# Routing weights of the PEER stage: added word by word into DRAM by indirect DMAs instead of built by one-hot products

## The chip, the core and the metric

The kernel runs on one core of one Trainium2 chip. The metric is the device time of one execution in microseconds, as a median of several executions; the profile is one execution more, recorded by the hardware profiler. A core has TensorE (PE, with a separate weight load, PEld), VectorE (DVE), ScalarE (ACT), GpSimd (POOL), SyncE (SP, which issues DMAs here) and 16 DMA engines. Each engine works through its instructions in the order of the program and waits on semaphores; it never takes a later instruction first.

## The reference, cut to what matters

One layer with three branches (differential attention, a chunk MLP, memory attention), a gate and an output projection, then PEER: every token picks 8 x 16 experts of 16384 by product keys and adds their weighted outputs. There are 320 tokens, 256 of the prompt and 64 samples.

```python
def _peer_block(xb, w_query, sub_keys, expert_u, expert_v):
    q = (xb @ w_query).reshape(tb, PEER_HEADS, 2, PEER_HALF)
    s = jnp.einsum('thpc,hpkc->thpk', q, sub_keys).astype(jnp.float32)
    s1, i1 = lax.top_k(s[:, :, 0], PEER_TOPK)
    s2, i2 = lax.top_k(s[:, :, 1], PEER_TOPK)
    ...
    top_s, top_j = lax.top_k(cand_s, PEER_TOPK)
    eidx = jnp.take_along_axis(cand_i, top_j, axis=-1)     # i1 * 128 + i2
    g = jax.nn.softmax(top_s, axis=-1).astype(xb.dtype)
    a = jax.nn.gelu(jnp.einsum('td,thkd->thk', xb, expert_u[eidx]), approximate=False)
    return jnp.einsum('thk,thkd->td', g * a, expert_v[eidx])
```

## The kernel before

**The stream.** All weights pass through one stream of *halves* of 512 KB (128 x 1024 words). SP loads a half into one of five `raw` buffers, ACT writes `hi` (the value rounded to the product format), DVE writes `lo` = `raw` - `hi`, and TensorE makes 24 products of a half: for each of 8 blocks `hi` by `xh`, `hi` by `xl`, `lo` by `xh`. There are four buffers each of `hi` and `lo`. The products of the stream stand at L359.

**PEER for the prompt.** The 256 prompt tokens are computed densely, over all 16384 experts. An Up piece (two halves of `pu`) gives 128 experts' activations for 256 tokens; four pieces are a group, with one buffer `hs` for GELU's output. There are 32 groups. The first 20 groups are written to DRAM (`hd`) and read back late. A Down piece (two halves of `pv`) takes the weighted activations `w` of two groups. 24 groups go up (192 halves) before the first Down piece; then Up and Down alternate until all 32 are up, and Down runs to the end.

**The routing weights G.** Ahead of Down, `weigh` multiplies `hs` by the weights `gg`, a table of 128 experts x 256 tokens for each piece. They come out of a DRAM array `gd`, which is filled during the first Up groups. Before, `weights_lane` runs 64 units (`g_unit`), four tokens each: DVE compares a row of 0 to 127 with the tokens' first and second key (`oa`, `ob`), GpSimd multiplies `ob` by the weight's two parts (`wH`, `wL`), TensorE makes 4 products of 128 x 256 (256 in all), ACT and DVE bring them into `st`, and SP writes `st` to `gd`, 1 MB for 16 tokens. When all units are through, SP loads `gg` from `gd`, 1 MB for two groups.

**PEER for the samples.** The 64 sample tokens use gathers: 128 indirect DMAs on GpSimd bring rows of `pur` into one of four buffers `gs` (128 rows of 4 KB), each followed by a dot product on DVE (`gs<-gs,xs`), then 128 of `pvr`, each followed by an addition into `x2s` on DVE. `idx` holds their row numbers.

**Routing.** `route_lane` finds the top 16 of the keys and of the pairs on DVE; `decode(i)` turns the results of one tile of tokens (0 and 1: prompt, 2: samples) into keys, weights and row numbers.

**What sets the order.** The program is written out by a planner (`Plan`): it keeps a clock for each engine and for DMA, with a cost for each instruction (a GpSimd gather 1.05 us, the DMA rate `RATE`, DVE's `dve_cost`, the gap `GAP` of a product), and lets the side tasks (routing, G, gathers, `weigh`) issue their instructions between the halves of the stream when its clocks say that their inputs are there. The planner's times are only used to order the instructions of each engine; on the chip every one waits on semaphores.

Of the kernel before, what the change touches and what calls it, by code (L numbers as in the profile page):

```python
# [11 lines left out]
F32 = mybir.dt.float32  # L12
# [9 lines left out]
TP = 256  # L22
# [15 lines left out]
RATE = 380e3  # L38
# [4 lines left out]
TB = 16  # L43
# [43 lines left out]
class Plan:  # L87
# [4 lines left out]
    def __init__(self):  # L92
        self.clk = {e: 0.0 for e in ("pe", "act", "dve", "pool", "dma")}
        self.task = self.main = Task(None)
        self.tasks = []
        self.done = {}
        self.uses = {}
        self.table = None

# [37 lines left out]
    def move(self, queue, out, src):  # L137

        at = max(self.last(out, True), self.last(src, False))
        if queue != "sync":  # L140
            at = self.clk[queue] = max(self.clk[queue], at) + (1.0 if queue == "pool" else 0.1)
        n = size(out) * out.shape[0] * 4
        self.clk["dma"] = max(self.clk["dma"], at) + n / RATE
        self.touch(out, self.clk["dma"] + 2.0, True)
        self.touch(src, self.clk["dma"] + 2.0, False)

    def gather(self, out, idx):
        at = self.clk["pool"] = max(self.clk["pool"], self.last(out, True), self.last(idx, False)) + 1.05
        self.clk["dma"] = max(self.clk["dma"], at) + size(out) * out.shape[0] * 4 / RATE
        self.touch(out, self.clk["dma"] + GLAT, True)  # L150
# [6 lines left out]
    def spawn(self, gen):  # L157
        self.tasks.append(Task(gen, self.task.at))
# [53 lines left out]
class Engine:  # L212
# [4 lines left out]
    def __getattr__(self, op):  # L217
        f = getattr(self.eng, op)

        def call(*a, **k):  # L220
# [4 lines left out]
            if op == "indirect_dma_start":  # L225
                p.gather(out, k["in_offset"].ap)
                return r
# [39 lines left out]
def hybrid_kernel(ctx: ExitStack, tc: tile.TileContext, ins, outs, stop=None):  # L267
# [34 lines left out]
    pool.memset(one, 1.0)  # L302
    mhalf = consts.tile([128, 1], F32, name="mhalf")
# [68 lines left out]
    class Piece:  # L372

        GAP = 0.0025
# [135 lines left out]

    s1 = ExitStack()
# [24 lines left out]
    def late_consts():  # L536
# [17 lines left out]
        dve.tensor_scalar(bgh, vec[:, V_BG:V_BG + 48], 0.5, None, op0=ALU.mult)  # L554

# [442 lines left out]
    spawn(late_consts())  # L998

# [131 lines left out]
    def open_route():  # L1131
# [5 lines left out]
        for n in ("iT0", "iT1", "wH", "wL"):  # L1137
            R[n] = p.tile([128, DN], F32R if n == "wH" else F32, name=n)
# [18 lines left out]
        spawn(weights_lane())  # L1157
# [45 lines left out]
    def wq_in(h, p):  # L1203
        def go(ps):
# [9 lines left out]
            if p == 1:  # L1214
                plan.see(sk)
                yield
                for i in range(3):
# [66 lines left out]
    def weights_lane():  # L1284
        yield from need(*[("dec", i) for i in range(3)])
        rtmp.close()
        q = open_pool(gtmp, "gtmp")
        OA = Slots(plan, q, "oa", [128, 4, 128], F32R, 3)
        OB = Slots(plan, q, "ob", [128, 4, 2, 128], F32R, 3)
        ST = Slots(plan, q, "st", [128, 128, TB], F32, 2)  # L1290
        st = None
        for t0 in range(0, DN, 4):
            if t0 % TB == 0:
                st, = yield from take(ST)
            oa, ob = yield from take(OA, OB)
            spawn(g_unit(t0, oa, ob, OA, OB, ST, st))
        while len(gdone) < DN // 4:
            yield
        gtmp.close()
        open_late()  # L1300
        mark("G")

    gdone = []
    gd = dram.tile([DN // TB, 128, 132 * TB], F32, name="gd")
    hd = dram.tile([NG, 128, GE * DN], F32, name="hd")

    def decode(i):
# [37 lines left out]
        rows = slice(0, 128) if i < 2 else slice(64, 64 + DN - TP)  # L1345
        n = rows.stop - rows.start
        if n:
            bk, = yield from take(BK)
            for a, nm in enumerate(("i0", "i1", "wt")):
                pe.transpose(bk[:, a * 128:a * 128 + n], R[nm][rows, i].rearrange("p h k -> p (h k)"), ident[rows, rows])  # L1350
            yield
            c = slice(i * 128, i * 128 + n)
            for a, nm in enumerate(("iT0", "iT1", "wH")):
                act.activation(R[nm][:, c], bk[:, a * 128:a * 128 + n], AF.Copy)
            dve.tensor_tensor(R["wL"][:, c], bk[:, 256:256 + n], R["wH"][:, c], op=ALU.subtract)
            BK.give(bk)
# [23 lines left out]

    def g_unit(t0, oa, ob, OA, OB, ST, st):

        io = cst[:, None, C_IO:C_IO + 128].to_broadcast([128, 4, 128])
        col = lambda nm: R[nm][:, t0:t0 + 4, None].to_broadcast([128, 4, 128])
# [4 lines left out]
        yield  # L1389
        b2 = yield from take(BK, BK)  # L1390
        for k in range(4):
            mm(b2[k // 2][:, (k % 2) * 256:(k % 2) * 256 + 256], oa[:, k, :], ob[:, k].rearrange("p j i -> p (j i)"),
               start=True, stop=True)
        OA.give(oa)
        OB.give(ob)
        yield
        o, work = t0 % TB, []
        for a, bk in enumerate(b2):
            v = bk.rearrange("p (t j i) -> p t j i", t=2, j=2)
            s2 = st[:, :, o + 2 * a:o + 2 * a + 2].rearrange("p i t -> p t i")  # L1400
            act.activation(s2, v[:, :, 0], AF.Copy)
            work.append((s2, v[:, :, 1], bk))
        yield
        for s2, x, bk in work:
            dve.tensor_tensor(s2, s2, x, op=ALU.add)
            BK.give(bk)
        if o == TB - 4:
            plan.see(st)
            yield
            sync.dma_start(gd[t0 // TB][:, :128 * TB], st.rearrange("p i t -> p (i t)"))  # L1410
            ST.give(st)
        gdone.append(t0)

# [10 lines left out]
    def open_late():  # L1424
        p = open_pool(late, "late")
        X["WT"] = Slots(plan, p, "w", [128, 2, 2 * GE, DN], F32R, 2)
        X["GG"] = Slots(plan, p, "gg", [128, DN // TB, 2 * GE * TB], F32, 1)

    def gathers():

        yield from need(("dec", 2))
        for src, use in (("pur", dot), ("pvr", axpy)):
            for j in range(128):
# [3 lines left out]
                spawn(use(j, gs))  # L1437
# [78 lines left out]
    def weigh():  # L1516
        for g in ORDER:
# [5 lines left out]
            h4 = hs.rearrange("p e (b t) -> p e b t", t=TB)  # L1523
            g4 = gg.rearrange("p b (e t) -> p e b t", t=TB)
            for k in range(GE + 1):
                if k < GE:
                    dve.tensor_tensor(h4[:, k], h4[:, k], g4[:, o + k], op=ALU.mult)
                    act.activation(w[:, 0, o + k, :], hs[:, k, :], AF.Copy)
                if k:
                    dve.tensor_tensor(w[:, 1, o + k - 1, :], hs[:, k - 1, :], w[:, 0, o + k - 1, :], op=ALU.subtract)  # L1530
                yield 0
# [208 lines left out]
```

## Time and profile before

| | us |
|---|---|
| median of 3 runs | 2733.84 |
| lowest and highest | 2730.56, 2739.34 |
| the profiled execution | 2734.69 |
| its span, first to last instruction | 2732.9 |
| granted TensorE clock, mean over the span | 0.985 |

The span falls into the earlier stages (0 to 1139.9), the Up groups ahead of the first Down product (1139.9 to 1797.4), the mixed and Down groups (to 2720.0), and an end of 12.9. Busy times count instructions at work; register, branch, semaphore and DMA-issuing instructions are not counted. A granted clock of 1.00 is 2.4 GHz for TensorE, the lower of its two levels is 1.2 GHz, and a mean between them is a share of time at each. A line "A <- B" among the waits is idle time of A that ended when B was done.

### The profile page before, as it was taken

How to read it: one execution, taken by the hardware profiler on the slowest of the kernel's cores; microseconds unless marked ns; L12 is line 12 of the kernel's file. 1: busy time of each engine (PE TensorE's matmuls, PEld its weight loads, DVE VectorE, ACT ScalarE, POOL GpSimd, SP SyncE). 2: the span in 40 equal slices, each digit the busy share in tenths (PEclk: the TensorE clock that was granted, in tenths of full speed). 3: DMA queues.
4: the chain of work that ended last, by engine and by line, in shares of the span. 5: the costliest groups of instructions: out<-in, count | busy, mean ns of one | idle time of the engine just before them, and what ended most of it. 6: DMA issues, size and time to landing. Idle time of an engine off the chain costs nothing. (4 is left out here: it accounts for less than half of the span.)

```text
span 2732.9 us, 49761 instructions
## 1 busy us (share of the span) xinstructions
PE 2633.5 (96%) x19824; PEld 2587.2 (95%) x19824; DVE 2024.8 (74%) x3201; ACT 1137.6 (42%) x1613; POOL 941.2 (34%) x728
## 2 busy tenths in 40 slices
PE   7999999999999999999889898999999999999998
PEld 5899989999999999999889898999999999999997
DVE  8545666344444449999999998888778888888887
ACT  4344444333333334344444444444444444344442
POOL 7423342000001222045878877422223321122122
PEclk9999999999999999999999999999999999999999
DMA  7433333444444554456777787798988888888887
GB/s 229 166 124 120 123 113 131 150 151 147 154 147 147 176 173 141 152 185 222 271 279 275 272 284 271 296 318 302 333 310 308 310 329 298 310 299 312 289 293 255
DMA packets 217560, 626.31 MB, mean 229 GB/s; under 512 B 19824, under 2 KB 74096, under 8 KB 215280
## 3 DMA queue, kind: packets, MB, share of 16 engines
q1 hardware_dynamic: 174944, 470.40, 49.1%
q0 software_dynamic: 39504, 142.24, 14.9%
q10 hardware_dynamic: 2880, 10.49, 1.0%
q8 instruction: 157, 2.57, 0.4%
q14 instruction: 75, 0.61, 0.1%
HBM read 589.36 MB, written 33.69 MB: 228 GB/s over the span
## 5 line engine op out<-in xcount | busy, mean ns | idle before, releaser
L221 DVE TENSOR_TENSOR lo<-raw,hi 128x1024 fp32r<-128x1024 f32 x792 | 1035.7, 1311 | 568.3 <-ACT hi L221 560.8
L221 ACT ACTIVATE hi<-raw 128x1024 fp32r<-128x1024 f32 x792 | 835.0, 1058 | 1106.1 <-PE mm L359 961.0
L359 PE MATMUL mm<-xb,hi 128*128 128x256 f32 x4096 | 758.6, 287 | 2.9 <-ACT hs L221 2.8
L359 PE MATMUL mm<-w,hi 128*128 128x256 f32 x4096 | 737.6, 283 | 0.0
L359 PEld LDWEIGHTS mm<-xb,hi 128*128 128x128 f32 x4096 | 654.4, 196 | 3.3 <-ACT hs L221 3.0
L359 PEld LDWEIGHTS mm<-w,hi 128*128 128x128 f32 x4096 | 639.0, 192 | 0.0
L359 PE MATMUL mm<-x_g,hi 128*128 128x320 f32 x2688 | 602.9, 313 | 0.0
L359 PE MATMUL mm<-xb,lo 128*128 128x256 f32 x2048 | 587.9, 287 | 0.8 <-DVE lo L221 0.8
L359 PE MATMUL mm<-w,lo 128*128 128x256 f32 x2048 | 579.6, 283 | 0.0
L359 PEld LDWEIGHTS mm<-x_g,hi 128*128 128x128 f32 x2688 | 447.2, 188 | 8.0 <-issue 3.9
L359 PE MATMUL mm<-x_g,lo 128*128 128x320 f32 x1344 | 415.7, 309 | 0.9 <-DVE lo L221 0.9
L359 PEld LDWEIGHTS mm<-xb,lo 128*128 128x128 f32 x2048 | 402.2, 196 | 1.3 <-DVE lo L221 1.2
L359 PEld LDWEIGHTS mm<-w,lo 128*128 128x128 f32 x2048 | 393.2, 192 | 0.0
L221 POOL DMA_INDIRECT gs<-pvr,idx x128 | 178.6, 1395 | 531.3 <-DVE x2s L221 525.4
L221 POOL DMA_INDIRECT gs<-pur,idx x128 | 188.9, 1476 | 223.0 <-DVE gs L221 199.6
L359 PEld LDWEIGHTS mm<-x_g,lo 128*128 128x128 f32 x1344 | 252.7, 188 | 1.2 <-DVE lo L221 1.2
L221 POOL TENSOR_TENSOR r<-r 128x320 f32<-128x320 f32 (+2 forms) x39 | 39.6, 1017 | 403.0 <-DVE r L221 398.4
L221 DVE SCALAR_TENSOR_TENSOR gs<-gs,xs 128x1024 f32<-128x1024 f32 x128 | 173.1, 1355 | 0.1
L221 DVE SCALAR_TENSOR_TENSOR x2s<-gs,act,x2s 128x1024 f32<-128x1024 f32 x128 | 163.7, 1279 | 1.8 <-DMA gs<-pvr,idx 1.5
L221 POOL TENSOR_TENSOR ob<-ob,wL 128x512 fp32r<-128x512 f32 x64 | 142.3, 2223 | 5.0
L221 DVE TENSOR_TENSOR r<-r,mm 128x256 f32<-128x256 f32 x256 | 106.3, 415 | 43.5 <-PE mm L359 43.4
L221 POOL TENSOR_TENSOR ob<-ob,wH 128x512 fp32r<-128x512 f32 x64 | 114.8, 1794 | 62.2 <-DVE ob L221 56.7
(246 smaller groups left out, 2730.3 us busy)
## 6 DMA issues: line engine op xcount, KB each, us to landing
raw<-pu SPq DMA_DIRECT2D x256, 512.0 KB
raw<-pv SPq DMA_DIRECT2D x256, 512.0 KB
raw<-win SPq DMA_DIRECT2D x168, 512.0 KB
raw<-wbr SPq DMA_DIRECT2D x32, 512.0 KB
raw<-wout SPq DMA_DIRECT2D x32, 512.0 KB
raw<-wq SPq DMA_DIRECT2D x32, 512.0 KB
gd<-st SPq DMA_DIRECT2D x16, 1024.0 KB
gg<-gd SPq DMA_DIRECT2D x16, 1024.0 KB
```

The lines of the kernel that those rows point to most:

```text
L221: r = f(*a, **k)
L359: nc.tensor.matmul(o, stays, moves, start=first, stop=last and n == len(products) - 1)
```

## The change

`g_unit` and `weights_lane` go. `gd` becomes one DRAM array for each prompt tile of 128 tokens, of 16 x 128 x 1024 words. `clear()` writes zeros into both by 32 DMAs on ACT's queue, 512 KB each, during the earlier stages. `decode` computes for the tiles 0 and 1 a word address for each token and pick (`ga`, six DVE operations, and `pt` once) and a copy of the weights (`gw`, GpSimd). `scatters()` then issues 256 indirect DMAs on GpSimd: 8 heads x 16 picks x 2 tiles, each adds 128 words, one for a token, into the array. A pair can be picked by two heads of one token, so the first DMA of a head waits for the 16 of the head before, in its tile. `weigh` works on whole groups (1024 wide) instead of quarters. `gg` is loaded by two DMAs of 512 KB, the first pair of which wait for all scatters. The samples' tile is routed first of the three. The additions into `x2s` are put ahead of other side tasks. The planner's numbers change: a lower DMA rate, kept for each queue; 0.0133 for the gap of a product; 0.16 for a DVE operation's fixed part; 1.05 for a scatter.

```diff
-RATE = 380e3
+RATE = 345e3
...
+    def scatter(self, idx, src):
+        at = self.clk["pool"] = max(self.clk["pool"], self.last(src, False), self.last(idx, False)) + 1.05
...
-    return max(0.107, n + 0.003) if op == "matmul" else 0.216
+    return max(0.107, n + 0.0133) if op == "matmul" else 0.216
...
-    return 0.07 + n / 0.96e3 * (6.2 if op == "reciprocal" else 1)
+    return 0.16 + n / 0.96e3 * (6.2 if op == "reciprocal" else 1)
...
+    def clear():
+        yield from need(("x",))
+        for q in range(NG // 2):
+            for g in gd:
+                act.dma_start(g[q].rearrange("p (a x) -> p a x", x=128), zeros[:, None, :].to_broadcast([128, 2 * GE, 128]))
+            at = plan.now() + 12.0
+            while plan.now() < at:
+                yield
...
+    def scatters():
+        yield from need(*[("ga", i) for i in range(DN // 128)])
+        for h in range(8):
+            for k in range(16):
+                for i in range(DN // 128):
+                    own = rounds.setdefault((h, i), [])
+                    j = 16 * h + k
+                    r = pool.indirect_dma_start(
+                        out=gd[i].rearrange("q p (x o) -> (q p x) o", o=1),
+                        out_offset=bass.IndirectOffsetOnAxis(ap=R["ga"][:, i, j:j + 1], axis=0),
+                        in_=R["gw"][:, i, j:j + 1], in_offset=None, compute_op=ALU.add)
+                    earlier = rounds[h - 1, i] if k == 0 and h else []
+                    after(r, earlier)
...
+            dve.tensor_scalar(u, b, 1.0, None, op0=ALU.mult)
+            dve.tensor_scalar(u, u, 3, None, op0=ALU.logical_shift_right)
+            dve.tensor_scalar(sf, u, 1.0, None, op0=ALU.mult)
+            dve.tensor_scalar(x, a, w8, R["pt"], op0=ALU.mult, op1=ALU.add)
+            dve.scalar_tensor_tensor(x, b, 128.0, x, op0=ALU.mult, op1=ALU.add)
+            dve.scalar_tensor_tensor(u, sf, 127.0 * w8, x, op0=ALU.mult, op1=ALU.add)
+            pool.tensor_copy(R["gw"][:, i], w.rearrange("p h k -> p (h k)"))
...
-    def g_unit(t0, oa, ob, OA, OB, ST, st):
-        dve.tensor_tensor(ob[:, :, 1, :], io, col("iT1"), op=ALU.is_equal)
-        pool.tensor_tensor(ob[:, :, 0, :], ob[:, :, 1, :], col("wH"), op=ALU.mult)
-        pool.tensor_tensor(ob[:, :, 1, :], ob[:, :, 1, :], col("wL"), op=ALU.mult)
-        dve.tensor_tensor(oa, io, col("iT0"), op=ALU.is_equal)
...
-                spawn(use(j, gs))
+                spawn(use(j, gs), use is axpy)
...
-            sync.dma_start(gg, gd[:, :, GE * TB * g:GE * TB * (g + 2)].rearrange("b p e -> p b e"))
+            for i in range(DN // 128):
+                r = sync.dma_start(gg[:, i].rearrange("p e t -> p (e t)"), gd[i][g // 2])
+                if g == ORDER[0]:
+                    after(r, rounds[7, i])
...
-            for k in range(GE + 1):
-                if k < GE:
-                    dve.tensor_tensor(h4[:, k], h4[:, k], g4[:, o + k], op=ALU.mult)
-                    act.activation(w[:, 0, o + k, :], hs[:, k, :], AF.Copy)
-                if k:
-                    dve.tensor_tensor(w[:, 1, o + k - 1, :], hs[:, k - 1, :], w[:, 0, o + k - 1, :], op=ALU.subtract)
+            dve.tensor_tensor(h4, h4, gg[:, :, o:o + GE].rearrange("p i e t -> p e i t"), op=ALU.mult)
+            act.activation(wh, hw, AF.Copy)
+            dve.tensor_tensor(wl, hw, wh, op=ALU.subtract)
```

On GpSimd, in the first Up groups of the kernel before, the weightings of `ob` and the gathers stand in turn:

```order
L221 TENSOR_TENSOR ob_15588<-ob_15588,wL 128x4x128
L221 DMA gs_15642<-pur,idx 128x1024
L221 TENSOR_TENSOR ob_15601<-ob_15601,wH 128x4x128
L221 TENSOR_TENSOR ob_15601<-ob_15601,wL 128x4x128
L221 DMA gs_15760<-pur,idx 128x1024
```

In the changed kernel the scatters stand there in one row; the four shown are the first of 256:

```order
L239 DMA gs_13254<-pur,idx 128x1024
L239 COPY gw<-wt 128x128
L239 DMA gs_13330<-pur,idx 128x1024
L239 DMA gd_89<-gw,ga 2097152x1
L239 DMA gd_90<-gw,ga 2097152x1
L239 DMA gd_89<-gw,ga 2097152x1
L239 DMA gd_90<-gw,ga 2097152x1
```

Only five gathers stand between the 256, behind 22, 36, 50, 64 and 176 of them; all others follow the last scatter.

On VectorE, where the gather behind 176 scatters (`gs_13892`) is used in the changed kernel, its dot stands behind `lo` of the Up half 134, with the `lo` of the next halves behind it:

```order
L239 TENSOR_TENSOR lo_15716<-raw_15564,hi_15715 128x1024
L239 TENSOR_TENSOR lo_15749<-raw_15594,hi_15748 128x1024
L239 SCALAR_TENSOR_TENSOR gs_13892,dots<-gs_13892,xs 128x1024
L239 TENSOR_TENSOR lo_15780<-raw_15626,hi_15779 128x1024
L239 TENSOR_TENSOR lo_15814<-raw_15656,hi_15813 128x1024
```

The dots of the gathers behind 22, 36, 50 and 64 scatters stand behind the halves 76, 82, 87 and 93, that of the first gather behind all 256 behind half 163. Before, dots stand all along, about nine in 16 halves.

On SP's queue of the kernel before, the last write of `st` and the first load of `gg` stand among the loads of `raw` like this, with 183 loads of Up halves ahead of `gg`:

```order
L221 DMA raw_18023<-pu 128x1024 [waits DMAHW5_49,DVE_49]
L221 DMA gd<-st_17569 128x2048
L221 DMA gg_18038<-gd 128x16x128 [waits DMAHW3_49,DMAHW4_49,PE_49,Pool_49]
L221 DMA raw_18062<-pu 128x1024 [waits DMAHW6_49,DVE_49]
L221 DMA raw_18095<-pu 128x1024 [waits DMAHW7_49,DVE_49]
```

In the changed kernel the first load of `gg` stands behind 169 such loads and waits on the eight semaphores (`DMASW`) of GpSimd's DMAs; these eight are taken in turn, so that a DMA of GpSimd waits for the one eight places ahead of it:

```order
L239 DMA raw_16629<-pu 128x1024 [waits DMAHW6_49,DMAHW3_49,DVE_49]
L239 DMA raw_16659<-pu 128x1024 [waits DMAHW7_49,DVE_49]
L239 DMA gg_16661<-gd_89 128x1024 [waits DMASW2_49,DMASW4_49,DMASW0_49,DMASW6_49,PE_49,Pool_49]
L239 DMA gg_16661<-gd_90 128x1024 [waits DMASW5_49,DMASW7_49,DMASW3_49,DMASW1_49]
L239 DMA raw_16696<-pu 128x1024 [waits DMAHW0_49,DVE_49]
```

## Rows read from the trace of the kernel before

**Rows 1.** Page, parts 1 and 2: busy time by engine; DMA share in 40 slices.
```profile
PE 2633.5 (96%) x19824; PEld 2587.2 (95%) x19824; DVE 2024.8 (74%) x3201; ACT 1137.6 (42%) x1613; POOL 941.2 (34%) x728
...
DMA  7433333444444554456777787798988888888887
```

**Rows 2.** Stretches: us, busy (instructions) by engine; clock, DMA share, GB/s.
```profile
core 0: us, PE busy (x) PEld busy (x) DVE busy (x) ACT busy (x) POOL busy (x), PEclk, DMA share, GB/s
1139.90:1797.40 657.50, 605.72 (x4798) 598.78 (x4797) 606.45 (x829) 301.90 (x438) 439.48 (x238) 0.96 0.74 262
1797.40:2720.00 922.60, 921.93 (x7684) 921.72 (x7682) 754.87 (x1026) 383.87 (x467) 227.39 (x172) 1.00 0.86 307
1139.90:1268.00 128.10, 123.18 (x1002) 122.70 (x1001) 116.73 (x242) 57.50 (x78) 45.51 (x28) 0.97 0.58 192
2650.00:2700.00 50.00, 50.00 (x419) 50.00 (x419) 42.05 (x48) 18.94 (x18) 13.80 (x13) 1.00 0.93 337
```

**Rows 3.** Tile `mm`, 1140 to 1800: ns min/median/max, first and last start.
```profile
L359 PE MATMUL mm<-xb,hi x3016: 274/283/583, 1139.9 to 1797.1; 128*128 128x256 f32 x189
...
L359 PE MATMUL mm<-w,hi x15: 283/283/283, 1797.4 to 1799.9; 128*128 128x256 f32 x15
```

**Rows 4.** Tile `ob`: its products.
```profile
L221 PE MATMUL bk<-ob,oa x256: 277/283/583, 1274.4 to 1736.8; 128*128 128x256 f32 x128
```

**Rows 5.** Waits of TensorE, 1139 to 1800: us, times, longest.
```profile
PE bk L221 <- POOL ob L221: 31.4, 10, 4.9
PE bk L221 <- DVE st L221: 14.2, 10, 3.8
PE mm L359 <- ACT hs L221: 2.8, 1, 2.8
PE bk L221 <- DVE i L221: 2.1, 1, 2.1
```

**Rows 6.** Page, part 5: the weightings of `ob` on GpSimd.
```profile
L221 POOL TENSOR_TENSOR ob<-ob,wL 128x512 fp32r<-128x512 f32 x64 | 142.3, 2223 | 5.0
...
L221 POOL TENSOR_TENSOR ob<-ob,wH 128x512 fp32r<-128x512 f32 x64 | 114.8, 1794 | 62.2 <-DVE ob L221 56.7
```

**Rows 7.** Chain that ended last, 1750 to 1800 and the end: start us, us, what.
```profile
1758.09 7.77 DMA raw<-pu
...
2721.25 5.14 DMA gs<-pvr,idx
...
2726.49 1.28 DVE x2s L221
```

**Rows 8.** Timeline of GpSimd, 2013 to 2018: start us, us, operation, idle before.
```profile
2014.63 0.95 POOL L221 DMA_INDIRECT gs<-pvr,idx  x1 [0.30 <-issue]
2015.89 0.95 POOL L221 DMA_INDIRECT gs<-pvr,idx  x1 [0.30 <-issue]
```

**Rows 9.** Tile `gs`: the gathers, ns min/median/max, first and last start.
```profile
L221 POOL DMA_INDIRECT gs<-pur,idx x128: 942/1262/5500, 1266.1 to 1993.1; - x128
...
L221 POOL DMA_INDIRECT gs<-pvr,idx x128: 947/948/2689, 2013.3 to 2721.3; - x128
```

**Rows 10.** Timeline of GpSimd: two gathers that start during a VectorE operation.
```profile
1319.14 1.77 POOL L221 DMA_INDIRECT gs<-pur,idx  x1 [0.30 <-DVE st L221]
...
2030.06 2.02 POOL L221 DMA_INDIRECT gs<-pvr,idx  x1 [0.64 <-DVE x2s L221]
```

**Rows 11.** Timeline of VectorE at the same times.
```profile
1318.88 1.21 DVE L221 TENSOR_TENSOR lo<-raw,hi 128x1024 fp32r<-128x1024 f32 x1
...
2030.04 1.22 DVE L221 TENSOR_TENSOR lo<-raw,hi 128x1024 fp32r<-128x1024 f32 x1
```

**Rows 12.** Tile `idx`: the operation that ends the routing of the samples.
```profile
L221 DVE TENSOR_SCALAR idx<-bk,cst x1: 346/346/346, 1265.5 to 1265.5; 128x128 uint32<-128x128 f32 x1
```

**Rows 13.** Waits of SP's queue, 1700 to 1800: us, times, longest.
```profile
SPq L221 <- DMA gd<-st: 10.1, 1, 10.1
```

**Rows 14.** Page, part 3: GpSimd's DMA queue.
```profile
q0 software_dynamic: 39504, 142.24, 14.9%
```

More of the change, by code (lines that the diff above doesn't have):

```diff
@@ L98, in __init__ @@
         self.table = None
+        self.queues, self.moved = {}, {}
     def now(self):
@@ L141, in move, with transfer @@
             at = self.clk[queue] = max(self.clk[queue], at) + (1.0 if queue == "pool" else 0.1)
[L142 to L145, printed above, removed]
+        end = self.transfer(queue, at, size(out) * out.shape[0] * 4)
+        self.touch(out, end + 2.0, True)
+        self.touch(src, end + 2.0, False)
     def gather(self, out, idx):
         at = self.clk["pool"] = max(self.clk["pool"], self.last(out, True), self.last(idx, False)) + 1.05
-        self.clk["dma"] = max(self.clk["dma"], at) + size(out) * out.shape[0] * 4 / RATE
-        self.touch(out, self.clk["dma"] + GLAT, True)
+        self.touch(out, self.transfer("gather", at, size(out) * out.shape[0] * 4) + GLAT, True)
+    def transfer(self, queue, at, n):
+        at = max(at, self.queues.get(queue, 0.0))
+        while n > 0:
+            k = int(at)
+            free = self.moved.get(k, RATE)
+            part = min(n, free, (k + 1 - at) * RATE)
+            self.moved[k] = free - part
+            n -= part
+            at = k + 1.0 if n > 0 else at + part / RATE
+        self.queues[queue] = at
+        self.clk["dma"] = max(self.clk["dma"], at)
+        return at
+    def scatter(self, idx, src):
+        at = self.clk["pool"] = max(self.clk["pool"], self.last(src, False), self.last(idx, False)) + 1.05
+        self.touch(src, at + 3.0, False)
+        self.touch(idx, at + 3.0, False)
     def see(self, *aps):
@@ L225, in call @@
             if op == "indirect_dma_start":
-                p.gather(out, k["in_offset"].ap)
+                if k["in_offset"] is None:
+                    p.scatter(k["out_offset"].ap, k["in_"])
+                else:
+                    p.gather(out, k["in_offset"].ap)
                 return r
@@ L508, in row_norm @@
         yield
+    gd = [dram.tile([NG // 2, 128, 2 * GE * 128], F32, name=f"gd{i}") for i in range(DN // 128)]
     s1 = ExitStack()
@@ L1216, in go @@
                 yield
-                for i in range(3):
+                for i in (2, 0, 1):
                     bk, = yield from take(BK)
@@ L1282, in route_lane, with late_lane, after @@
                     spawn(decode(i))
-    def weights_lane():
+    def late_lane():
         yield from need(*[("dec", i) for i in range(3)])
         rtmp.close()
[L1287 to L1297, printed above, removed]
+        open_late()
+    rounds = {}
+    def scatters():
[11 more added lines that the diff above has]
+                    after(r, earlier)
+                    tc.declare_no_dep(r.ins, group=f"tile{i}", reason="other words", keep=[x.ins for x in earlier])
+                    own.append(r)
+                    tc.add_to_no_dep_group(f"tile{i}", r.ins)
+                yield 0
+        at = plan.clk["pool"] + 5.0
+        while plan.now() < at:
             yield
-        gtmp.close()
-        open_late()
         mark("G")
-    gdone = []
-    gd = dram.tile([DN // TB, 128, 132 * TB], F32, name="gd")
+    def after(r, others):
+        for x in others:
+            tc.add_manual_dep(r.ins, x.ins.name, mybir.DependencyInfo(mybir.DependencyClass.Sync, mybir.DependencyReason.DATA),
+                              reason="adds to the same words")
     hd = dram.tile([NG, 128, GE * DN], F32, name="hd")
@@ L1344, in decode @@
         R["XT"].give(zs)
[L1345 to L1356, printed above, removed]
+        if i < DN // 128:
+            w8 = 2.0 * GE * 128
+            a, b = (R[nm][:, i].rearrange("p h k -> p (h k)") for nm in ("i0", "i1"))
+            xs_, = yield from take(R["XT"])
+            sf, x = xs_[:, 0:128], xs_[:, 128:256]
+            u = R["ga"][:, i]
+            if i == 0:
+                dve.scalar_tensor_tensor(x, ident, 1.0, cst[:, C_IO:C_IO + 128], op0=ALU.mult, op1=ALU.mult,
+                                         accum_out=R["pt"])
+                mark("pt")
+            else:
+                yield from need(("pt",))
+            dve.tensor_scalar(u, b, 1.0, None, op0=ALU.mult)
[5 more added lines that the diff above has]
+            pool.tensor_copy(R["gw"][:, i], w.rearrange("p h k -> p (h k)"))
+            R["XT"].give(xs_)
+            mark("ga", i)
         if i == 2:
```

54 lines of the change are left out of this document (17 added, 37 removed).

## Prediction

> **What bounds the kernel now.** I read the busy shares first [rows 1]: TensorE works 96% of the span, so a gain has to come out of TensorE's own work, its waits or its clock. Then the stretches of the PEER part [rows 2]. From the first Up product at 1139.9 to the first Down product at 1797.4 [rows 3] there are 657.5 us; from there to the end of the products 922.6 us. The Down stretch is TensorE back to back: 922.60 / 7684 = 0.120 us for a product at granted clock 1.00, so a half (24 products) takes 2.88 us. The Up stretch is not. Its 192 halves (24 groups of 4 pieces of 2 halves, 4608 products) at 0.120 would be 553 us; it takes 104.5 more. These are, by rows: 256 one-hot products, 256 x 0.12 = 30.7 us [rows 4]; TensorE's waits in this stretch for GpSimd's one-hot operands, 31.4, and for the additions into `st`, 14.2, with some 5 of other waits [rows 5]; and the clock: a mean of 0.96 in 657.5 us [rows 2] is some 53 us at the lower level (1.2 GHz) instead of 2.4, which costs half of that, 26. The sum, 107, overlaps a little. Behind TensorE, GpSimd is the busiest of the helpers here: 439 us, of which the 128 two-part weightings of `ob` are 142.3 + 114.8 [rows 6].
>
> **What the change removes.** All 256 products, the weightings and both waits. What stays of the surplus is what the routing itself costs: in 1139.9 to 1268.0, ahead of the first one-hot product at 1274.4 [rows 4], 1002 products took 128.1 us [rows 2], 1002 x 0.120 = 120.2, so 8 us; in the changed order the routing is spread over 64 halves where it had 46, so I take 12. The Up stretch without any new wait is then 553 + 12 = 565, a gain of 92. The end gains too: before, four last `x2s` additions and a gather stand behind the last product [rows 7], 2720.0 to 2732.9; with the additions put ahead of other work (`urgent`) the last of them stands 20 halves earlier, and of these 12.9 us some 5 stay (an output transfer), a gain of 8. The weighting of `h` in whole groups saves some DVE overhead, in a stretch where TensorE does not wait for DVE: nothing. The 32 clears of 512 KB go into the stretch of the earlier stages, where the DMA row of the page shows 3 to 5 tenths [rows 1]; nothing, +-6 for the moved order there. The span without stalls: 2732.9 - 92 - 8 = 2633.
>
> **What it adds.** 256 accumulating indirect DMAs on GpSimd, all behind one another, and no gather, except five, between them. No row shows such a DMA. The nearest rows are the gathers, which also hand 128 indices to GpSimd. Four of them one behind the other start every 1.25 us (0.95 of work and 0.30 that the profile calls issue) [rows 8]. But the median of the `pur` gathers is 1262 ns, not 948 [rows 9], and [rows 10, 11] show why: a gather that starts while a DVE operation with two SBUF inputs runs does not end before some 0.82 us after that operation (`lo` from 1318.88 to 1320.09, gather from 1319.14 to 1320.91; `lo` from 2030.04 to 2031.26, gather from 2030.06 to 2032.08). With one `lo` of 1.22 us [rows 11] per half of 2.88 us, two starts fit into a half: one falls into `lo` and ends 0.82 after it, the next starts 0.30 later, ends 0.95 later, and the third would start again in the next `lo`. So **a slot is 1.44 us while TensorE runs, and 1.25 us while it stands still.** I take these for a scatter. To that come seven turns of a round, where a scatter waits for the DMAs of the round before: between 0 and a gather's landing less a slot, 5.14 [rows 7] - 1.44 = 3.7 us; I take 2 (a word is less than a row of 4 KB).
>
> The Trainium skill ("SBUF — State Buffer", Who interferes with whom) says that a DVE tensor_tensor with two SBUF inputs contends only with GpSimd instructions that read SBUF, and that descriptor generation, which needs the write interface, is not held (inferred there). By that a slot would be 1.25 us throughout. The trace speaks against it [rows 10, 11]: `lo` is such an operation, and the gathers are held.
>
> **Where the scatters meet the rest.** I count from the first Up product, U. The order puts the address operations of the second tile behind `lo` of Up half 64. DVE runs some 8 us ahead of TensorE, so that is 64 x 2.88 + 12 - 8 = 188, with the operations themselves about U+190. Before, `idx` stood behind half 46 at 1265.5, U+126 [rows 12]. The gathers' dots on DVE are where it comes back. DVE works in order, and a dot that waits for its gather holds all `lo` behind it, and so TensorE:
> - The dot behind half 93 reads a gather that stands behind 64 scatters and 4 others: 190 + 68 x 1.44 + 2 + 5 = 295; DVE is there at 93 x 2.88 + 4 = 272. 23 us late, 8 covered by the `lo` made ahead: some 17 stall.
> - The dot behind half 134 reads one behind 176 scatters, slot 181. DVE is there at 134 x 2.88 + 4 + 17 = 407. Since 190 have passed 217 us, less 10 of turns; 145 slots done. 36 at 1.25, a turn and the landing: 45 + 2 + 6, less 8: 45 to 47.
> - The dots behind half 163 on read gathers behind all 256. DVE is there at 163 x 2.88 + 4 + 64 = 537. From 457 on, 76 us without turns give 53 slots; of 261 some 27 are left: 34 + 7 (a gather and its landing) less 8: 33.
>
> So the scatters end about U+571 and the stall is 17 + 47 + 33 = **97 us**. SP's queue adds its own wait at the same place: the first `gg` load stands behind 169 loads of `raw`, and waits for all scatters; the loads behind it (half 170, due at 170 x 2.88 + 12 + 64 = 566) wait with it. Before, the same mechanism shows with `gd<-st`: 10.1 us on SP [rows 13], and a stretch of the chain that waits for a `raw` load, 7.77 [rows 7]. Here it lies within the third stall, give or take 5. The granted clock is 0.96 in the stretch with waits and 1.00 in the one without [rows 2]; many short waits cost 26 us there, and three long ones I put at 4.
>
> In the Down stretch some 60 more gathers, with their dots, fall behind the first Down, since GpSimd gave 380 us to scatters. DMA goes from 0.86 to about 0.93; at 0.93 and 337 GB/s TensorE was still fully busy (50.00 of 50 us) [rows 2], and DVE had 754.87 of 922.6, plus 60 dots of 1.22 is 828. Nothing, with 20 us as the upper end.
>
> **The sum:** 2633 + 97 + 4 = 2734 us of span; the profiled execution took 1.8 us more than its span and stands 0.9 above the median, so about **2735**, +0.05%. What is gained comes back almost whole.
>
> **Rivals.**
> 1. *The slot is short*, near the 1.05 us that the planner books. 190 + 261 x 1.05 + 14 = 478, ahead of U+487, when load 169 is due: the scatters stay hidden but for some 5 to 20 us: 2640 to 2655. For it: a scatter moves one word, and its work could be less than a gather's 0.95. Against: the number of indices is the same, and 0.30 of each gather is issue. With 1.25 throughout, that is, if `lo` does not hold a scatter as it holds a gather, the same walk gives 0 + 30 + 30, a stall of 60, 2697. Together faster: 0.36. The rule of the Trainium skill named above ("SBUF — State Buffer", Who interferes with whom) would lead to this second case.
> 2. *A word costs the DMA rings more than GpSimd.* q0 shows 39504 packets at 14.9% of 16 engines over 2732.9 us [rows 14]: 0.149 x 16 x 2732.9 / 39504 = 165 ns for a packet of mostly 4 KB. A scatter has 128 words, 8 for an engine; an accumulating word must be read and written. From 1.44 / 8 = 180 ns per word the rings decide, not GpSimd. At 250 ns a slot is 2.0 us: scatters end at 190 + 512 + 14 + 5 = U+721, TensorE gets to half 170 at 501, a stall of some 230: 2865, slower. At 200 ns (1.6 us) some 130: 2768. The same times come from 0.2 to 0.5 us more work per scatter on GpSimd, whose gather has a plain source. For it: nothing in the trace accumulates, and each scatter waits, before it starts, for the DMA eight places earlier on the queue's semaphores, so that a delay in the rings becomes GpSimd's. Against: a word is far less to move than 4 KB. Chance of slower by this: 0.36.
>    The Trainium skill ("DMA: Bandwidth & Descriptors", Specifications) says that transfers under 512 bytes are done by read-modify-write, without a time; no run here shows one yet.
> 3. *The Down stretch or the turns take more*: +8 to +25 by the upper ends above (turns of 3.7: 12; DMA or DVE in the Down stretch: 20): 2743 to 2760, slower. 0.10.
> 4. *The forecast itself*, within 0.3% (2726 to 2742): 0.18.
>
> **How the numbers follow.** About 0.3% (8 us) is what a measurement of this kernel can tell from no change. Faster 0.36, same 0.18, slower 0.46 (0.36 + 0.10). The point is the likeliest walk, 2735; its own range, by slots of 1.35 to 1.5 and turns of 0 to 3.7, is 2715 to 2760. The range for 8 in 10 leaves out a tenth on either side: below, a fully hidden scatter (under 2655), above, words at 250 ns and more: 2655 to 2860.
>
> **What would show it.** The first Down product against U: U+662 by the sum (565 + 97), U+570 to 590 if hidden, over U+690 if the rings decide. Scatters on GpSimd: 0.95 work and 0.30 between them, longer where a `lo` runs; if the rings decide, GpSimd's idle time ahead of a scatter is put down to a DMA. Between half 82 and half 170 TensorE's waits should be for `lo`, and DVE's for gathers. The stretch behind the first Down product should still be 0.120 us a product. It is wrong if U moves by over 6 us, or if TensorE stalls with GpSimd done.

## The result and the profile after

The changed kernel takes 2894.78 us (median of 4 runs, 2892.66 to 2895.56) against 2736.59 before: a ratio of 1.0579, interval 1.0557 to 1.0602. It is 158 us slower, above the upper end of the range, 2860. The stretches of the profiled execution (span 2893.7), first Up product to first Down product and from there to the end of the products; the columns are those of [rows 2]:

```profile
1128.40:1982.00 853.60, 576.10 (x4650) 574.26 (x4650) 383.17 (x663) 240.76 (x301) 578.92 (x337) 0.83 0.58 161
1982.00:2890.00 908.00, 908.00 (x7684) 907.99 (x7682) 786.72 (x932) 374.43 (x380) 280.81 (x212) 1.00 0.91 335
```

and the same first stretch of the kernel before, from its first Up product on:

```profile
1129.10:1797.40 668.30, 616.52 (x4888) 609.58 (x4887) 617.25 (x881) 307.52 (x443) 440.20 (x240) 0.96 0.74 261
```

The Up stretch grows from 668.3 to 853.6 us, by 185; the Down stretch falls from 922.6 to 908.0, by 15; the end behind the last product from 12.9 to 3.7, by 9. With the first Up product at 1128.4 instead of 1129.1 these make the 161 us between the spans. TensorE's work in the Up stretch is gone as forecast (4650 instructions instead of 4888), and so are the waits of [rows 5]. In their place stand others. The waits of TensorE and of VectorE, 1120 to 2000 (us in total, times, longest):

```profile
PE mm L382 <- DVE lo L239: 268.8, 7, 126.6
PE bk L239 <- DVE xt L239: 6.0, 1, 6.0
PE mm L382 <- ACT hs L239: 2.7, 1, 2.7
```

```profile
DVE gs L239 <- DMA gs<-pur,idx: 310.3, 7, 133.7
```

TensorE stands 268.8 us for `lo`, and VectorE, in whose queue `lo` stands, waits 310.3 us at seven dots for gathers (133.7 at the longest). Those gathers stand behind scatters. TensorE's three longest waits, as its timeline has them (start of the product behind the wait, us, operation, idle before):

```profile
1389.12 0.58 PE L382 MATMUL mm<-xb,lo 128*128 128x256 f32 x1 [17.50 <-DVE lo L239]
1723.35 0.58 PE L382 MATMUL mm<-xb,lo 128*128 128x256 f32 x1 [126.62 <-DVE lo L239]
1899.35 0.58 PE L382 MATMUL mm<-xb,lo 128*128 128x256 f32 x1 [90.73 <-DVE lo L239]
```

The first belongs to the dot behind half 76; those behind 82, 87 and 93 cost 11.5, 12.1 and 8.5 more, so that the four make 49.6. The other two belong to the dots behind half 134 and behind half 163. SP's queue waits for scatters at the last of them too (1330 to 2010):

```profile
SPq L239 <- DMA gd<-gw,ga: 94.6, 3, 87.8
```

The scatters and gathers (ns min/median/max, first and last start), to compare with [rows 9]:

```profile
L239 POOL DMA_INDIRECT gd<-gw,ga x256: 1546/1547/2618, 1332.2 to 1889.8; - x128
```

```profile
L239 POOL DMA_INDIRECT gs<-pur,idx x128: 936/938/1960, 1278.6 to 2271.5; - x128
```

A scatter takes GpSimd 1547 ns where nothing is in its way, a gather 938; 256 of them stretch over 1332.2 to 1889.8, 2.19 us each. Timelines of GpSimd (start us, us, operation, idle before) and of VectorE while TensorE runs, to compare with [rows 10, 11]:

```profile
1563.01 2.58 POOL L239 DMA_INDIRECT gd<-gw,ga  x1 [0.30 <-issue]
1565.89 2.58 POOL L239 DMA_INDIRECT gd<-gw,ga  x1 [0.30 <-issue]
1568.77 2.58 POOL L239 DMA_INDIRECT gd<-gw,ga  x1 [0.30 <-issue]
```

```profile
1562.94 1.23 DVE L239 TENSOR_TENSOR lo<-raw,hi 128x1024 fp32r<-128x1024 f32 x1 [1.65 <-ACT hi L239]
1565.82 1.23 DVE L239 TENSOR_TENSOR lo<-raw,hi 128x1024 fp32r<-128x1024 f32 x1 [1.66 <-ACT hi L239]
1568.70 1.22 DVE L239 TENSOR_TENSOR lo<-raw,hi 128x1024 fp32r<-128x1024 f32 x1 [1.66 <-ACT hi L239]
```

and of GpSimd while TensorE and VectorE stand, to compare with [rows 8]:

```profile
1651.97 1.55 POOL L239 DMA_INDIRECT gd<-gw,ga  x1 [0.30 <-issue]
1653.82 1.55 POOL L239 DMA_INDIRECT gd<-gw,ga  x1 [0.31 <-issue]
1655.67 1.55 POOL L239 DMA_INDIRECT gd<-gw,ga  x1 [0.30 <-issue]
```

Beside a `lo` a scatter takes 2.58, and with 0.30 of issue it starts 2.88 us after the one before: once in a half, in step with `lo`. Standing, the period is 1.85.

### The profile page after: what moved, and what is told of

Same layout as the page of the kernel before. It is cut to its first block, busy times and chain, and to the rows that moved or that the text cites. A ratio compares the mean times of both kernels' runs of the same rounds, so it can differ in the third digit from the quotient of the medians.

```text
span 2893.7 us, 48601 instructions
## 1 busy us (share of the span) xinstructions
PE 2581.8 (89%) x19562; PEld 2540.7 (88%) x19562; DVE 1801.3 (62%) x2765; ACT 1059.9 (37%) x1384; POOL 1119.5 (39%) x858
## 5 line engine op out<-in xcount | busy, mean ns | idle before, releaser
L239 DVE TENSOR_TENSOR lo<-raw,hi 128x1024 fp32r<-128x1024 f32 x792 | 999.9, 1265 | 655.1 <-ACT hi L239 644.9
L382 PE MATMUL mm<-xb,lo 128*128 128x256 f32 x2048 | 588.1, 287 | 268.8 <-DVE lo L239 268.8
L382 PE MATMUL mm<-w,hi 128*128 128x256 f32 x4096 | 723.9, 279 | 0.0
L382 PEld LDWEIGHTS mm<-w,hi 128*128 128x128 f32 x4096 | 627.3, 188 | 0.0
L239 POOL DMA_INDIRECT gd<-gw,ga x256 | 469.7, 1835 | 83.2 <-issue 76.8
L382 PEld LDWEIGHTS mm<-w,lo 128*128 128x128 f32 x2048 | 384.4, 188 | 0.0
L239 DVE SCALAR_TENSOR_TENSOR gs<-gs,xs 128x1024 f32<-128x1024 f32 x128 | 157.8, 1234 | 310.3 <-DMA gs<-pur,idx 310.3
L239 POOL DMA_INDIRECT gs<-pvr,idx x128 | 196.2, 1533 | 332.0 <-DVE x2s L239 317.2
L239 POOL DMA_INDIRECT gs<-pur,idx x128 | 141.6, 1106 | 271.6 <-DVE gs L239 263.2
L382 PE MATMUL mm<-x2g,hi 128*128 128x320 f32 x512 | 114.4, 310 | 0.0
```

The costliest lines, as they stand in the source:

```text
L239: r = f(*a, **k)
L382: nc.tensor.matmul(o, stays, moves, start=first, stop=last and n == len(products) - 1)
```

## The experiments

A run without a ratio is one execution. On one chip 19 executions of the kernel before lie between 2728.9 and 2741.8 us, so a difference below some 15 us is not read from such a run.

**Without the scatters.**

```diff
-                    r = pool.indirect_dma_start(out=gd[i]..., compute_op=ALU.add)
-                    ...
+                    continue
```

> The changed kernel without its 256 scatters (the weights stay zero, so the prompt's PEER part is left out of the result); the clears, the loads of gg and all other work stay. Theory: all of the stall of 269 us comes from the scatters, and what is left is 1128 to the first Up product, about 570 Up, 908 Down and 4: 2610 to 2620. Rival: a part of the stall is from the gathers' new places: over 2640.

2613.44 us, span 2611.7. The stretches:

```profile
1128.50:1699.90 571.40, 560.90 (x4650) 560.29 (x4649) 458.81 (x793) 240.90 (x301) 170.51 (x146) 0.99 0.83 300
1699.90:2608.00 908.10, 908.10 (x7684) 908.10 (x7682) 720.88 (x802) 373.99 (x380) 199.02 (x147) 1.00 0.81 297
```

So all of the loss hangs on the scatters: without them Up takes 571 us. Their price is 281 us. Whether the gathers' new places cost something by themselves, this run can't tell: without scatters the planner writes the dots 14 to 16 in every 20 Up halves again, where the changed kernel has only one between the halves 100 and 160. For the Down stretch the changed kernel tells it: with the late gathers it takes 908.0 us, here 908.1.

**Is it the adding?**

```diff
-                        in_=R["gw"][:, i, j:j + 1], in_offset=None, compute_op=ALU.add)
+                        in_=R["gw"][:, i, j:j + 1], in_offset=None)
```

> The 256 indirect DMAs write their words instead of adding them (a pair picked twice by a token keeps one weight, so the sum is left out); all else as in the changed kernel. There each took GpSimd 1.547 us where nothing on VectorE disturbs it, a gather 0.94. Theory A: the adding costs GpSimd the 0.6 us more. Then these take 0.95, a slot 1.25 to 1.44, the stall shrinks from 269 us to about 97 and the time is about 2715. Theory B: it is the write of single words into an addressed DRAM array, adding or not. Then 1.55 each, and about 2895 as before.

2919.95 us, slower still, but for another reason. What the run was for, GpSimd's time for one of them:

```profile
L239 POOL DMA_INDIRECT gd<-gw,ga x256: 962/968/1980, 1332.0 to 1680.6; - x128
```

0.968 us, as a gather. Theory A holds for GpSimd: writing words costs it what a gather does, and the adding 0.58 us more. Theory A's time was wrong, since a second limit shows. The last write starts at 1680.6, 209 us earlier than the last scatter, and yet the first Down product comes at 2006.6, 25 us later than with scatters. TensorE's waits, and a stretch in which VectorE waits for nothing of GpSimd:

```profile
PE mm L382 <- issue: 258.1, 134, 3.8
```

```profile
1500.00:1660.00 160.00, 21.17 (x57) 16.39 (x57) 2.45 (x2) 2.50 (x3) 120.51 (x125) 0.50 0.05 10
```

All engines but GpSimd get next to nothing done, DMA moves 10 GB/s, and TensorE's products come one by one, 2.8 us apart, each with "issue" ahead of it. GpSimd's 125 instructions in these 160 us stand 1.28 us apart.

**The same writes at a slower pace.**

```diff
+                    pool.tensor_tensor(R["gx"], R["gx"], R["gx"], op=ALU.add)
```

behind each plain write.

> Plain writes as in the run with plain writes, each followed by an unneeded addition of 128x128 on GpSimd (some 0.86 us), so that they start at the pace of the adding ones. With plain writes back to back TensorE stood on its own issue for 258 us and DMA moved 12 GB/s between 1500 and 1680. Theory: that comes from the pace, one 128-word DMA in 1.27 to 1.44 us being more than the DMA engines finish; at 2.1 us or more they keep up, TensorE waits for lo again, and the time is 2830 to 2900. Rival: plain word writes hold up the DMA engines at any pace: TensorE stands on issue again, 2900 or more.

2752.8 us, less than either expectation. The writes start 1.9 us apart in the mean (1332.2 to 1818.8; most of the gaps are 1.6 to 1.8 or 2.4), and the standstill is gone. The stretch of above, and TensorE's waits:

```profile
1500.00:1660.00 160.00, 160.00 (x1336) 160.00 (x1335) 69.04 (x56) 66.10 (x84) 141.79 (x165) 1.00 0.61 203
```

```profile
PE mm L382 <- ACT w L239: 104.0, 1, 104.0
PE mm L382 <- DVE lo L239: 20.2, 5, 8.7
```

That speaks for the pace: 1.28 us apart the plain writes hold everything up, 1.9 apart (83 in these 160 us) they don't. The planner had put the dots and gathers elsewhere in this kernel, so that the pace is not the only thing that differs. What fails at 1.28 us stays open: in the standstill the DMA engines are recorded as busy for 5% of the time, and the queues that bring instructions moved 2 packets, where the paced run has 13 and the changed kernel 10 in the same stretch; that can be the cause or the effect.

The rival of the rings is settled by the changed kernel's own trace. 1.85 us a scatter is the fastest that occurs there, and its scatters waited for a scatter's DMA for 6.1 us in all (six waits). The queue of GpSimd's DMAs there, 1500 to 1660, with 70 scatters and nothing else (packets, MB, share of 16 engines):

```profile
q0 software_dynamic: 10071, 0.04, 15.4%
```

0.154 x 16 x 160 us are 394 us of the engines' time for 70 x 128 words, 44 ns a word, where the rival needed 180.

**Does `lo` hold the scatters?**

```diff
-            dve.tensor_tensor(lo, raw, hi, op=ALU.subtract)
+            if 60 <= self.n_up <= 192 and isinstance(p, Up):
+                act.activation(lo, raw, AF.Copy)
+            else:
+                dve.tensor_tensor(lo, raw, hi, op=ALU.subtract)
```

> For the Up halves 60 to 192 lo is made by ScalarE, by a copy of raw (so the remainder is left out and Up's values are wrong there); VectorE then runs no operation with two SBUF inputs beside the scatters but the five dots. Theory: a scatter that starts during a lo is held until 0.82 us after it, so that one slot fits a half of 2.88 us while TensorE runs, and 1.85 while it stands. Without lo on VectorE all slots are 1.85: the scatters take 256 x 1.85 + turns = 485 us instead of 558, the longest ones of 2.58 us are gone, and the stall falls by 60 to 80 us: about 2820. Rival: the long ones come from TensorE's or DMA's traffic: then they stay at 2.58, and the time at about 2895.

2818.54 us. The scatters stretch over 1323.8 to 1815.4, 1.93 us each instead of 2.19, and where TensorE runs they now read

```profile
1501.29 1.55 POOL L239 DMA_INDIRECT gd<-gw,ga  x1 [0.30 <-issue]
1503.14 1.55 POOL L239 DMA_INDIRECT gd<-gw,ga  x1 [0.30 <-issue]
1505.00 1.55 POOL L239 DMA_INDIRECT gd<-gw,ga  x1 [0.31 <-issue]
```

1.55 and 1.85 apart, where they were 2.58 and 2.88, with TensorE busy all the time from 1490 to 1510. `lo` on VectorE is what holds them. Without the hold the kernel takes 76 us less; the row of scatters is 66 us shorter, and the planner had also put the dots elsewhere. The other part, GpSimd's own 1.85 us by 256, stays, and it is paid at another place, on SP's queue, where raw loads stand behind the first `gg` load (SP's waits and TensorE's):

```profile
SPq L239 <- DMA gd<-gw,ga: 219.0, 3, 213.4
```

```profile
PE mm L386 <- ACT hi L239: 205.3, 1, 205.3
```

TensorE stands there with Up halves still ahead of it, so that the first Down product comes at 1905.1, 90 us behind the last scatter; in the run with the paced writes, whose last one starts 3 us later, it comes at 1830.1.

**GpSimd's time, or the places of the dots?**

```diff
-        at = self.clk["pool"] = max(...) + 1.05
+        at = self.clk["pool"] = max(...) + 2.88
```

in the planner's `scatter`.

> The changed kernel with the planner's cost of a scatter at 2.88 us, the period measured beside lo, instead of 1.05: dots and the loads of gg are written where their data really come. Theory: GpSimd's time for 256 scatters is the bound, not the dots that wait in VectorE's queue. TensorE then runs through to the end of its 192 Up halves at about 1128 + 575 = 1703 with some 130 scatters done (372 us at 2.88), and stands there for the rest, 126 at 1.85 and the turns, 240 to 250 us: about 2865. Rival: the dots' places make the stall: 2620 to 2680.

2869.94 us. With the true cost the planner writes no dot ahead of its data, TensorE runs through Up, and then stands once:

```profile
PE mm L382 <- ACT w L239: 248.4, 1, 248.4
```

The wait moves from `lo` to the first `w`, from 268.8 to 248.4 us, and the time falls by 25 of the 281 us. It does not fall further, since TensorE now runs through Up, and beside `lo` the scatters are slow: the last one starts at 1935.1, 45 us later than before. The dots decide in the main where the bill is paid. With this planning, half the scatters:

```diff
-            for k in range(16):
+            for k in range(8):
```

> The changed kernel with the planner's cost of a scatter at 2.88 and only the first 8 of 16 picks of each head scattered (the other weights are left out of the result). Theory: GpSimd's time is the bound; 128 scatters at 2.88 from 204 us behind the first Up product on end about 575 us behind it, as Up does, so that the stall of 248 us all but vanishes: 2615 to 2640. Rival: the stall comes from something that does not go with the number of scatters (turns, the first gg, the order): over 2700.

2631.63 us (half of the weights are left out). The scatters, and TensorE's longest wait:

```profile
L239 POOL DMA_INDIRECT gd<-gw,ga x128: 1547/2575/2619, 1330.4 to 1691.7; - x128
```

```profile
PE mm L382 <- ACT w L239: 16.0, 1, 16.0
```

128 scatters of 2.58 end at about 1694, and the stall goes with the number.

**The other parts of the change, alone.** The kernel before with the planner's numbers, the order of routing, the `x2s` additions put first and `weigh` in whole groups:

```diff
-RATE = 380e3
+RATE = 345e3
...
-                spawn(use(j, gs))
+                spawn(use(j, gs), use is axpy)
...
-            for k in range(GE + 1):
+            dve.tensor_tensor(h4, h4, g4[:, o:o + GE], op=ALU.mult)
```

> The kernel before with the planner's new numbers, the samples' tile routed first, the additions into x2s put first and weigh in whole groups; the one-hot products stay, without clears and scatters. Theory: the parts beside the scatters gain by themselves, the Down part 14 us (0.118 us a product instead of 0.120) and the end 9, and the Up part stays at 668: about 2712. Rival: the faster Down part comes from what the one-hot products leave free in SBUF or in the order: then Down stays at 922 and the time is about 2727.

2750.28 us, ratio 1.0065 (1.0046 to 1.0084): a loss, against both expectations. Down keeps 0.120 us a product, and TensorE waits for the first `w`, for which it did not wait before:

```profile
PE mm L372 <- ACT w L234: 25.0, 1, 25.0
```

So the parts beside the scatters don't gain by themselves, and the faster Down part is not theirs.

**What makes Down faster.** Before, a product with `xb` or `w` takes 0.120 us at granted clock 1.00; in the changed kernel one with `w` takes 0.118 (908.0 / 7684) and one with `xb` 0.120. The instructions are the same; the buffers lie elsewhere. First all of them were moved by 32 bytes, which changed nothing:

```diff
+    pad = consts.tile([128, 8], F32, name="pad")
```

> The kernel before with one unused tile of 32 bytes per partition ahead of its buffers; nothing else. In the kernel before w begins at byte 155040 of a partition, 32 past a multiple of 64, and a Down product takes 0.120 us in every case; in the changed one w begins at 153536, a multiple of 64, and it takes 0.118; xb is 32 past in both, and there both take 0.120. Theory: the product's moving operand is read faster where it begins at a multiple of 64 bytes. Then Up's and Down's products both take 0.118, 12288 x 0.0022 = 27 us less: about 2705, and less still if the products of 320 columns gain too. Rival: something else in the changed kernel, then about 2733 as before.

2733.90 us, ratio 0.9996 (0.998 to 1.0011), 0.120 for both: the rival's time. With the `x2s` additions put first as well:

> As the one before, and the additions into x2s put ahead of other side tasks (the planner's costs as in the kernel before). Theory: the end behind the last product goes from 12.9 to about 4 us, for 9 us less than the run with the 32 bytes alone: about 2696. Rival: the additions then stand in the way of weigh or lo, and the gain is nothing or a loss.

2743.55 us, ratio 1.0026 (1.0014 to 1.0038), 10 us above the run before it instead of 9 below: the last addition starts at 2729.7, behind the last product at 2718 as before. Putting the additions first doesn't clear the end when the planner's costs stay.

Then the buffers behind `hi` and `lo` were moved, and `hi` and `lo` not:

```diff
+    pad = ab.tile([128, 8], F32, name="pad")
```

> The kernel before with an unused tile of 32 bytes per partition behind the buffers of hi and lo: hi and lo begin 32 past a multiple of 64 bytes as before, x_g, xb and w, which begin behind the tile, at a multiple of 64. In the run that moved all of them together nothing changed, 0.120 us a product. Theory: it is the two operands' places against one another that count; 32 bytes apart (modulo 64), as w and hi are in the changed kernel, a product of 256 columns takes 0.118. Then Up and Down gain 12288 x 0.0022 = 27 us, and products of 320 columns perhaps another 10: 2695 to 2708. Rival: it comes from what the changed kernel does beside the products: 2733.

2711.36 us, ratio 0.9909 (0.9881 to 0.9938). The Down stretch:

```profile
1802.60:2702.60 900.00, 899.08 (x7684) 898.34 (x7682) 748.38 (x1023) 383.05 (x467) 254.70 (x172) 1.00 0.87 313
```

900.0 instead of 922.6, with 7684 instructions as in [rows 2]: 0.117. Up's products fell to 0.117 as well, but that stretch, 667.7, did not get shorter: TensorE's busy time in it fell by 8.7 us (616.5 to 607.8), and its waits grew from 51 to 59 (22.2 for `ob` and 22.9 for `st`). The products of 320 columns stayed at 0.147. So the places of the two operands against one another count; by which rule, the last two runs tell in part.

The places are not all that counts. In the run with the true cost of a scatter every buffer of these products lies where the changed kernel has it, and yet its products with `w`, at 0.118 at first as there, get faster on the way. The same stretch of Down in the changed kernel and in that run:

```profile
2500.00:2700.00 200.00, 200.00 (x1700) 200.00 (x1700) 181.63 (x205) 82.35 (x78) 70.28 (x46) 1.00 0.94 353
2500.00:2700.00 200.00, 200.00 (x1716) 200.00 (x1715) 182.42 (x206) 85.68 (x82) 73.25 (x45) 1.00 0.93 347
```

1700 products in 200 us are 0.1176 each, 1716 are 0.1166.

**A version that beats both.** The first 128 prompt tokens by scatters, the other 128 by one-hot units whose weightings run on VectorE, the 32 bytes behind `lo`. Ahead of each scatter stands a memset of one word a partition on GpSimd, and the planner books 2.6 us for a scatter; neither was tried alone. From the edit against the changed kernel:

```diff
-                for i in range(DN // 128):
+                for i in range(1):
+                    pool.memset(R["tick"], 0.0)
...
+    def g_unit(t0, oa, ob, OA, OB, ST, st):
...
+        dve.tensor_tensor(ob[:, :, 0, :], ob[:, :, 1, :], col("wH"), op=ALU.mult)
+        dve.tensor_tensor(ob[:, :, 1, :], ob[:, :, 1, :], col("wL"), op=ALU.mult)
```

> A mixture for the whole result: the weights of the first 128 prompt tokens by 128 adding scatters (planned at 2.6 us each), those of the other 128 by 32 one-hot units, whose weightings run on VectorE instead of GpSimd; and the 32 bytes behind hi and lo. Theory: 128 scatters fit beside the Up part, as half of them did, and the one-hot half costs TensorE 128 products, 15 us, and no waits for GpSimd: 1127 to the first Up product, 576 + 15 + some 20 of waits for VectorE less 13 by the operands' places, 900 Down, 4: about 2630, up to 2650 where is_equal and the weightings hold the scatters. Rival: VectorE's many operations with two SBUF inputs hold the scatters so long that Down waits again, 50 us or more: over 2680.

2645.22 us, ratio 0.9676 (0.966 to 0.9693), 89 us less than before. The stretches:

```profile
1123.50:1717.70 594.20, 567.92 (x4782) 566.06 (x4780) 478.80 (x825) 272.15 (x368) 368.39 (x325) 0.98 0.75 236
1717.70:2639.20 921.50, 920.19 (x7680) 919.61 (x7681) 805.18 (x989) 374.58 (x380) 296.21 (x223) 1.00 0.91 336
```

Up takes 594 us; the 128 scatters lie in 1325.7 to 1672.3, and TensorE's only longer wait is 10.2 us for the first `w`. Down stayed at 0.120 here, though `w` and `hi` are 32 bytes apart modulo 64. Modulo 128 they are 96 apart, and 32 in the kernels with 0.117 and 0.118. So `w` was moved by 64 bytes:

```diff
+        p.tile([128, 16], F32, name="pad2")
```

> The mixture with 64 bytes more ahead of w. In the mixture xb begins 32 bytes behind hi modulo 128 and a product takes 0.117 us, w begins 96 bytes behind hi modulo 128 and it takes 0.120, though modulo 64 both are the same; in the kernels with 0.117 to 0.118 for w it begins 32 behind modulo 128. Theory: 32 modulo 128 is the place that counts; with w there too, Down's 6144 products gain 0.003 each, 19 us: about 2626. Rival: the place is no cause, and the time stays at 2645.

2640.21 us, ratio 0.9649 (0.9622 to 0.9675), the fastest that computes the whole result. The Down stretch:

```profile
1719.80:2635.40 915.60, 912.30 (x7682) 911.30 (x7682) 802.01 (x990) 374.34 (x380) 329.37 (x223) 1.00 0.92 338
```

A Down product takes 0.119, not 0.117: a part of what was expected, and the two ratios' intervals overlap. The place counts, and the rule isn't settled.

## Why the prediction was wrong

- **The slot of a scatter is the term that was mis-sized.** The prediction took a gather's 0.95 us. The adding one takes 1.547. The mechanism around it was right in each part: the hold by `lo`, the dots in VectorE's order as the place where TensorE stands, their order, SP's `gg` load as a second wait (94.6 us for scatters on SP, beside the third stall). But 1.547 + 0.30 is 1.85 while TensorE stands, not 1.25; and beside `lo` only one slot fits a half, 2.88, and not two of 1.44. So the forecast's stall of 97 us became 268.8: 49.6 at the dots behind the halves 76 to 93 instead of 17 (its own terms give 15, 23 less 8), 126.6 behind half 134 instead of 47, 90.7 behind half 163 instead of 33.
- **The no-stall span** was 2633 forecast and 2611.7 measured (without the scatters). A misreading is in it: [rows 3] come from a view that begins at 1140, and their 1139.9 was taken for the first Up product. It stands at 1129.1, as the row of 668.3 us above shows. The Up stretch before was longer by 10.8 than reckoned, but without the scatters it took 571.4 and not 565, so that the gain of the change in it was 97 and not 92 (668.3 to 571.4). Of the 21 us that is 5. Down gained 14.5 (922.6 to 908.1), which nothing in the prediction held; it goes with the faster products with `w`. The rest is the end and the start.
- **The hold by `lo`** had been read right from two gathers: with `lo` on ScalarE the same scatters fell from 2.58 to 1.55. The Trainium skill ("SBUF — State Buffer", Who interferes with whom) infers that such an operation doesn't hold descriptor generation. These runs speak against that inference: indirect DMAs on GpSimd are held by it (2.58 beside `lo`, 1.55 without).
- **The rival that came in** is the second, by its side sentence: 0.2 to 0.5 us more work per scatter on GpSimd. It was 0.6 more. Its main form, the rings as the limit, did not: 6.1 us of waits for scatters' DMAs, and 44 ns a word. The upper end of the range was set at 2.0 us a slot, a value between the 1.85 and the 2.88 that occur; with the hold by `lo` applied to that rival too, its slot would have been 2.88 beside `lo`, and its time near the measured one. That was the fault of the range: the rival was worked out with a flat slot, without the hold that the forecast itself had found.
- **The clock** cost more than the 4 us that the forecast gave it. The same 4650 instructions kept TensorE busy for 576.1 us in the Up stretch, and 560.9 without the scatters: 15 us. Behind a long wait a product takes 0.58 us, as in the timeline above, where the median is 0.283. The mean granted clock of 0.83 is mostly of time in which TensorE stands.
- **Smaller terms.** The first scatter starts 204 us behind the first Up product (190 forecast). The end fell to 3.7 (5 forecast). The turns cost 6.1 us in all (14). The Down stretch took the additional gathers without loss, at a DMA share of 0.91.

## What to carry to other kernels

An instruction that the trace has never shown is not priced by its nearest relative alone: the adding DMA cost GpSimd 1.6 times the gather, and since a VectorE operation that comes in every half held it, the step from 0.95 to 1.55 doubled its period from the 1.44 that the forecast had worked out to 2.88. Where a mechanism makes time go in steps, work out each rival with it and look how far the next step is. Where an engine's total (256 x 1.85 = 474 us, or 737 beside `lo`) doesn't fit the stretch that is to hide it (some 368 us from the first scatter to the end of Up), moving the waiting instructions mostly moves the wait (25 us of 281 gained); giving half the work to other engines made it fit.

## What the runs showed that was not expected

- Single words written by indirect DMAs 1.28 us apart went with an all but stopped core: 10 GB/s and a product every 2.8 us between 1500 and 1660. In the run with 1.9 us between them, 203 GB/s and no idle time of TensorE in that stretch. Why is open.
- The places of a product's two operands in SBUF count: 0.120 us where they begin at the same place modulo 64 bytes, 0.117 to 0.118 in several layouts with the moving operand 32 bytes behind modulo 128; 96 behind gave 0.120, and one layout with 32 behind 0.119. One and the same layout gave 0.1176 in one run and 0.1166 in another, so something else counts too. 6144 products at 0.003 are 18 us. Products of 320 columns did not change. Why is open.
